# Down phases of four passes by a 26-product algorithm, with its w_down operands made beside earlier passes

## Chip, cores, metric

One core of a Trainium2 chip. The metric is the device time of one execution in microseconds (us).

## Reference

x is 8 x 1024 x 1024, w_gate and w_up 1024 x 4096, w_down 4096 x 1024, all fp32:

```python
gate = x @ w_gate
up = x @ w_up
gate = 0.5 * gate * (1 + np.tanh(np.sqrt(2 / np.pi) * (gate + 0.044715 * gate ** 3)))
h = gate * up
return (h @ w_down).astype(np.float32)
```

## The kernel before

Eight passes of 1024 tokens, counted from 0. Each pass has a gate/up phase and a down phase. Operands are fp16. The down phase multiplies h (1024 x 4096) by w_down with seven products of a Strassen scheme: 7 x 2 x 4 x 8 = 448 matmuls of 512 columns. I call 8 of them, one group below, a slot (1.73 us). Parts, with cuts marked "...":

```python
def cast_x(p):                      # fp32 -> fp16 through the DMA, on GpSimd's queue
    r = slice(p * TOK, (p + 1) * TOK)
    nc.gpsimd.dma_start(out=xh[r, :], in_=x2[r, :])

def transpose_x(p):                 # four DMA transposes, on SyncE's queue
    for n, kh, mh in (("b11", 0, 0), ("b21", 1, 0), ("b12", 0, 1), ("b22", 1, 1)):
        r0 = p * TOK + mh * MH
        nc.sync.dma_start_transpose(
            out=xq[n], in_=xh[r0 : r0 + MH, kh * MH : (kh + 1) * MH]
        )
...
def gate_up_fast(p):                # passes 3 to 7: 8 quads of 26 products of 8 matmuls
    owed = {}
    for q in range(NQ):
        extra = {}
        if q == 2 and p + 1 < NPASS:
            extra[3] = [lambda: cast_x(p + 1)]
        ...
DSEQ = ["P1", "P2", "P6", "P5", "P7", "P3", "P4"]
def down(p):
    ...
    for v, name in enumerate(DSEQ):
        ...
        for nb in range(2):
            kc = 2 * v + nb
            dc = d_chunk(p, kc)                     # w_down operand, in a ring of six chunks
            for g in range(G):
                for n in range(8):
                    nc.tensor.matmul(ps_all[:, bank[b, g]], lhs[...], dc[:, n, :], ...)
                ...
                if nb == 1:
                    if name == "P1":                # ScalarE copies bank a to bank c;
                        bank["c", g] = ps_free.popleft()   # P2 goes on in bank c
                        nc.scalar.copy(ps_all[:, bank["c", g]], ps_all[:, bank["a", g]])
                    ...
                for s in sums.get((name, nb, g), ()):
                    hsum(*s)                        # VectorE: sums of h
                if nb == 0 and g == 0 and p + 1 < NPASS:
                    ...
                    if v == (2 if p < FAST - 1 else 0):     # FAST = 3
                        transpose_x(p + 1)
                if v >= (5 if p < FAST - 1 else 3) and work:
                    work.popleft()()                # VectorE: scaling and sums of next x
            ...
                if kc == 0 and p < FAST:
                    for k in range(3, 6):
                        load_d(p, k)                # ring loads, SyncE's queue
                load_d(p, kc + 6)
```

All loads, stores and transposes but the casting ones are issued by SyncE, in program order. And ScalarE's copy from bank a to bank c stands between product P1 and product P2: TensorE needs it at slot 8, 13.8 us into the phase.

## Time and profile before

| | before |
|---|---|
| median of 3 runs | 2290.01 us (2289.75 to 2291.56) |
| TensorE in a down phase | 96.69 us, no wait |
| TensorE in a fast gate/up phase | 181.65 us, no wait |

The chain of the kernel before and its stages are in the prediction. One more view of it is needed: SyncE's timeline where down phase 2 begins (it begins at 795.30). Columns: start and duration in us, engine, line, operation, what is moved, how many.

```profile
795.37 8.98 SPq L178 DMA_TRANSPOSE x_b<-x_half  x4
804.45 11.92 SPq L396 DMA_DIRECT2D ring<-wd_ops  x6
```

The four transposes of the next x hold SyncE's queue for 9.0 us; the ring loads of the phase come behind them, and in time.

### The profile page before, as it was taken

Reading aid. Unit: us, or ns where it says so; the run is one execution under the profiler, and the core shown is the slowest. Engines: PE = TensorE matmul, PEld = TensorE weight load, DVE = VectorE, ACT = ScalarE, POOL = GpSimd, SP = SyncE. Lnnn points to the kernel's source line nnn. Section 1 sums busy time; section 2 is a strip of 40 time slices with the busy share of each in tenths; the row PEclk is TensorE's granted clock in tenths of the full one; section 3 lists DMA queues with packets and bytes.
Section 4 is the critical chain, followed back from the end, with each engine's and each line's share of the span. In section 5 each row is a group of like instructions: output and inputs, shape, how many; then the busy total and the mean of one; then the engine's idle time right before and its main releaser. Section 6 shows DMA issues by size and latency. Waiting matters only on the chain.

```text
span 2287.4 us, 38185 instructions
## 1 busy us (share of the span) xinstructions
PE 2276.5 (100%) x14719; PEld 1437.7 (63%) x14719; DVE 1342.2 (59%) x1946; ACT 958.6 (42%) x1860; POOL 676.4 (30%) x818
## 2 busy tenths in 40 slices
PE   9999999999999999999999999999999999999999
PEld 4444444444444446887468874788648886488854
DVE  5576367772587744677346673466735677256650
ACT  4443135551355513555135641455404553055620
POOL 1342013230133301454024540254303452044520
PEclk9999999999999999999999999999999999999999
DMA  9998959888899977988579885798858987588752
GB/s 239 175 207 211 254 144 225 215 255 250 182 220 225 266 245 258 308 287 263 203 263 317 275 275 193 265 319 277 268 194 273 311 284 253 198 279 281 268 210 108
DMA packets 258054, 557.20 MB, mean 244 GB/s; under 512 B 74768, under 2 KB 134160, under 8 KB 243728
## 3 DMA queue, kind: packets, MB, share of 16 engines
q1 hardware_dynamic: 204992, 483.46, 62.1%
q0 software_dynamic: 52880, 71.31, 18.8%
q8 instruction: 115, 1.88, 0.4%
q14 instruction: 67, 0.55, 0.1%
HBM read 512.75 MB, written 113.25 MB: 274 GB/s over the span
## 4 chain that ended last, share of the span: by engine, by line
PE 97%; DVE 2%; issue 0%; DMA 0%; ACT 0%; SPq 0%; DVEq 0%; ACTq 0%
PE ps L681 40%; PE ps L793 34%; PE ps L474 23%; PE ps L877 1%; DVE ring L273 1%; DVE tmp L493 0%; DMA h_a<-in_x_dram 0%; DVE h_a L511 0%; DVE x_sums L201 0%; DVE h_s L334 0%; DVE h_s L336 0%; DVE h_s L338 0%; ACT x_b L229 0%; DVE x_b L228 0%; SPq L217 0%
## 5 line engine op out<-in xcount | busy, mean ns | idle before, releaser
L681 PEld LDWEIGHTS <-ring 128*128 128x128 f16 x8320 | 814.1, 98 | 95.2
L658 POOL TENSOR_TENSOR h_a<-tmp 128x256 f16<-128x256 f32 x640 | 465.5, 747 | 927.4 <-ACT tmp L646 893.5
L681 PE MATMUL ps<-x_sums,ring 128*128 128x256 f16 x5760 | 655.8, 273 | 0.0
L793 PE MATMUL ps<-ring,h_a 128*128 128x512 f16 x2944 | 638.4, 379 | 0.0
L643 DVE TENSOR_TENSOR tmp<-tmp,ps 128x512 f32<-128x512 f32 x640 | 413.8, 683 | 220.4 <-PE ps L681 168.3
L793 PEld LDWEIGHTS <-h_a 128*128 128x128 f16 x3072 | 300.6, 98 | 361.4
L474 PEld LDWEIGHTS <-ring 128*128 128x128 f16 x2632 | 257.5, 98 | 314.5 <-issue 4.7
L628 ACT COPY tmp<-ps 128x512 f32<-128x512 f32 x520 | 304.4, 585 | 203.9 <-PE ps L681 128.9
L474 PE MATMUL ps<-x_sums,ring 128*128 128x512 f16 x1504 | 341.0, 379 | 3.0 <-DVE ring L273 2.0
L646 ACT ACTIVATE tmp<-tmp 128x256 f32<-128x256 f32 x640 | 263.8, 418 | 172.7 <-DVE tmp L641 80.0
L732 ACT ACTIVATE tmp<-ps 128x512 f32<-128x512 f32 x128 | 76.4, 597 | 587.2 <-PE ps L793 587.2
L681 PE MATMUL ps<-x_b,ring 128*128 128x256 f16 x2560 | 305.6, 273 | 0.0
L500 POOL TENSOR_TENSOR h_a<-tmp 128x512 f16<-128x512 f32 x94 | 150.4, 1600 | 375.1 <-ACT tmp L498 286.1
L474 PE MATMUL ps<-x_b,ring 128*128 128x512 f16 x1128 | 259.1, 379 | 0.0
L641 DVE TENSOR_TENSOR tmp<-ps,tmp 128x512 f32<-128x512 f32 x240 | 165.4, 689 | 151.4 <-ACT tmp L628 104.2
L736 DVE SCALAR_TENSOR_TENSOR tmp<-ps,tmp 128x512 f32<-128x512 f32 x64 | 44.2, 690 | 303.4 <-ACT tmp L732 260.3
L493 DVE TENSOR_TENSOR tmp<-ps,tmp 128x512 f32<-128x512 f32 x188 | 127.0, 683 | 137.5 <-ACT tmp L485 134.6
L485 ACT COPY tmp<-ps 128x512 f32<-128x512 f32 x188 | 110.1, 586 | 92.2 <-PE ps L474 89.7
L740 DVE TENSOR_TENSOR h_a<-h_a,h_a 128x2048 f16<-128x2048 f16 x96 | 111.2, 1215 | 58.1 <-PE ps L793 58.1
L273 DVE TENSOR_TENSOR ring<-ring 128x1024 f16<-128x1024 f16 x188 | 132.7, 721 | 6.9 <-PE ps L793 3.8
L498 ACT ACTIVATE tmp<-tmp 128x512 f32<-128x512 f32 x94 | 58.8, 626 | 146.6 <-DVE tmp L493 146.6
L793 PE MATMUL ps<-ring,h_s 128*128 128x512 f16 x480 | 104.9, 379 | 0.0
(68 smaller groups left out, 798.6 us busy)
## 6 DMA issues: line engine op xcount, KB each, us to landing
ring<-w_ops SPq DMA_DIRECT2D x480, 512.0 KB, 4.5
ring<-wd_ops SPq DMA_DIRECT2D x105, 1024.0 KB, 5.4
out_dram<-tmp SPq DMA_DIRECT2D x128, 256.0 KB, 2.5
w_ops<-x_sums SPq DMA_DIRECT2D x110, 256.0 KB, 6.3
ring<-in_w_gate_dram POOLq DMA_DIRECT2D x23, 1024.0 KB, 9.9
ring<-in_w_up_dram POOLq DMA_DIRECT2D x23, 1024.0 KB, 18.0
w_ops<-h_s SPq DMA_DIRECT2D x82, 256.0 KB, 5.5
x_half<-in_x_dram POOLq DMA_DIRECT2D x7, 2048.0 KB, 15.7
```

The lines of the kernel that those rows point to most:

```text
L273: nc.vector.tensor_tensor(o, a, b, op)
L474: nc.tensor.matmul(ps(b, w), lhs[:, k], rhs[:, k, :], start=(first and k == 0), stop=(k == KH - 1), skip_group_check=True,)
L493: nc.vector.tensor_tensor(o, ps("b", w), o, ADD)
L500: nc.gpsimd.tensor_tensor(hq[TO[n]][:, i, :], tmp[:, t[n, 1]], tmp[:, t[n, 0]], MUL)
L628: nc.scalar.copy(tmp[:, t[o[1]]], ps_all[:, bank[o[2]]])
L641: nc.vector.tensor_tensor(d, b, a, SUB)
L643: nc.vector.tensor_tensor(d, a, b, ADD if o[4] == "add" else SUB)
L646: nc.scalar.activation(d, d, GELU, scale=GSC)
L658: nc.gpsimd.tensor_tensor(h, tmp[:, t[o[1]], MQ : 2 * MQ], g, MUL)
L681: nc.tensor.matmul(ps_all[:, bank[c], w * MQ : (w + 1) * MQ], lhs[:, w, k], rhs[:, k], start=(first and w == 0 and k == 0), stop=(k == KH ...
L740: nc.vector.tensor_tensor(hq[o][:, s, :], hq[a][:, s, :], hq[b][:, s, :], op)
L793: nc.tensor.matmul(ps_all[:, bank[b, g]], lhs[:, j, g * P : (g + 1) * P], dc[:, n, :], start=(first and j == 0), stop=(j == NP - 1), skip_ ...
```

## The change

Intent: in passes 4 to 7 the down phase becomes `down_fast`, an algorithm with 26 products of 32 matmuls of 256 columns (832 matmuls) where the plain product of these blocks has 32. It needs 24 operands of 1 MB that are sums of blocks of w_down. They are made once, in eight units, beside passes 2 to 4: two units each in down phases 2 and 3 and in gate/up phases 3 and 4. The core of the diff, cut (the lists of sums and products and most of `down_fast` are left out):

```diff
+    def wd_unit(u, raw, free):
+        ...
+        def load():
+            for k, c, v in ((0, 0, 0), (1, 0, 1), (1, 1, 5)):
+                nc.sync.dma_start(out=blk[:, k, c], in_=wdop[2 * v + nb][:, j : j + 2, :])
+            nc.gpsimd.dma_start(out=blk[:, 0, 1], in_=wd_eo[0][:, 2 * u : 2 * u + 2, HH:])
+        ...
+        def step(i):                      # 19 of them
+            stores()                      # to DRAM, SyncE's queue
+            n, op, a, b = WD_SUMS[i]
+            v = at[n] = free.popleft()
+            combine(node(n), op, node(a), node(b))       # VectorE
+            ...
+            if i % 3 == 0 and i // 3 < len(plain):
+                m, sign = plain[i // 3]
+                v = free.popleft()
+                nc.scalar.activation(..., node(m), COPY, scale=float(sign))   # ScalarE
 ...
     def gate_up_fast(p):
+        if p in UNITS_UP:
+            free = deque(hf["s3"][:, 4096 + j * 512 : 4608 + j * 512] for j in range(8))
+            for i, u in enumerate(UNITS_UP[p]):
+                load, fs = wd_unit(u, hf["s3"][:, 0:4096], free)
+                steps[i * 78] = load
+                for k, f in enumerate(fs):
+                    steps[i * 78 + 14 + 3 * k] = f
 ...
+    UNITS_DOWN = {2: (0, 1), 3: (4, 5)}
+    UNITS_UP = {3: (2, 3), 4: (6, 7)}
 ...
     def down(p):
+        if p in UNITS_DOWN:
+            free = deque(xc[:, j * 512 : (j + 1) * 512] for j in range(24, 38))
+            for i, u in enumerate(UNITS_DOWN[p]):
+                load, fs = wd_unit(u, xc[:, i * 8192 : i * 8192 + 4096], free)
+                steps[i] = [load]
+                for k, f in enumerate(fs):
+                    steps.setdefault(3 + 19 * i + k, []).append(f)
 ...
                         if v == (2 if p < FAST - 1 else 0):
                             transpose_x(p + 1)
-                    if v >= (5 if p < FAST - 1 else 3) and work:
+                    for f in steps.get((2 * v + nb) * G + g, ()):
+                        f()
+                    if v >= x_from and work:
                         work.popleft()()
 ...
-        down(p)
+        if p < DFAST:                     # DFAST = 4
+            down(p)
+        else:
+            down_fast(p)
```

In a gate/up phase a slot is 8 matmuls of 256 columns, 0.873 us, and a phase has 208 of them.

## The prediction

> **What bounds the kernel now.** I read the list of the critical chain in order of time first, then the busy times of each engine by stage, then timelines of the moments where a down phase begins. The kernel has eight passes of 1024 tokens; each is a gate/up phase and a down phase. From pass 2 on (passes are counted from 0) the chain is nothing but TensorE:
>
> ```profile
> 795.30 96.69 PE ps L793 x448
> 891.99 181.65 PE ps L681 x1664
> 1073.65 96.69 PE ps L793 x448
> 1170.34 181.65 PE ps L681 x1664
> ...
> 2005.38 181.65 PE ps L681 x1664
> 2187.03 96.71 PE ps L793 x448
> ```
>
> Columns: start, duration, engine and line, instructions. L793 is a down phase (7 products, 448 matmuls of 512 columns), L681 a fast gate/up phase (1664 matmuls of 256 columns). Each piece starts where the last ended: no wait anywhere. So time saved in TensorE's instruction stream counts in full, and each new wait counts in full. From these rows, a 512-column matmul takes 96.69/448 = 0.2158 us, a 256-column one 181.65/1664 = 0.10917 us.
>
> The stages (passes 3, 5 and 7):
>
> ```profile
> core 0: us, PE busy (x) PEld busy (x) DVE busy (x) ACT busy (x) POOL busy (x), PEclk, DMA share, GB/s
> 891.99:1073.65 181.66, 181.66 (x1666) 162.77 (x1664) 120.37 (x190) 106.99 (x230) 88.28 (x125) 1.00 0.86 292
> 1351.99:1448.69 96.70, 96.70 (x451) 43.92 (x449) 41.74 (x50) 12.63 (x23) 5.31 (x5) 1.00 0.66 215
> 2187.03:2283.70 96.67, 96.67 (x449) 43.63 (x446) 26.87 (x27) 12.64 (x23) 5.32 (x5) 1.00 0.39 140
> ```
>
> VectorE (DVE) and the DMA are far from full in a down phase; in the gate/up phase the DMA share is 0.86. That is where the change has to find room.
>
> [...]halving the columns costs about 2.5 ns per extra matmul. [...]the trace's h sums of that size take 1215. [...]four such sums beside GpSimd take 5.87 us, eight without it 9.16 (1.47 against 1.15 each). [...]the busiest fortieth of this trace moves 319[...].
>
> **The change, part by part.**
>
> *TensorE.* A down phase of passes 4 to 7 becomes 26 products of 16 x 2 matmuls of 256 columns: 832 x 0.10917 = 90.83 us for 96.69. Saved 5.86 us a pass, 23.4 us in four. Weight loads (98 ns each) must hide under 109 ns, as they already do in L681. 2290.0 - 23.4 = 2266.6 is the floor.
>
> *VectorE in the new phase.* 18 sums of 128x4096 f16; none exists yet. Rows of 1024 and 2048 elements take 683 and 1215 ns, so an estimate by that slope is 2.28 us: 41.0 us. 24 reads of PSUM at 0.69: 16.6. 23 operations for the next pass's x (21 near 0.69, 2 of 1.22): 16.8. Together 74.4 of 90.8 us. A product lasts 32 x 0.109 = 3.49 us; by the program's list no slot holds more than about 3.0 us of VectorE work except two with 4.6, each with light neighbours, and each sum stands about one slot ahead of its use.
>
> *Start of that phase.* In pass 5 GpSimd is still multiplying h when the phase starts at 1351.99:
>
> ```profile
> 1350.49 6.81 POOL L658 TENSOR_TENSOR h_a<-tmp 128x256 f16<-128x256 f32 x7 [1.20 <-ACT tmp L646]
> ```
>
> It ends 5.3 us in. The first two products leave their last two rows for later: 56 matmuls, 6.1 us. That holds. The first sum waits for the fourth from last multiplication (some 2.5 us in) and the second for the last; they end near 5.5 and 8, and are needed at 10.5 and 14.0.
>
> *Making the operands.* Eight units, each 19 sums of 128x512 f16 (0.42 us, estimated from 683 - 266), six ScalarE copies (0.6), four loads and 24 stores of 128 KB. Two units go into the down phases of passes 2 and 3 and into the gate/up phases of passes 3 and 4. On average it fits: 16 us of VectorE on 120.4 of 181.7, or on 41 of 96.7. The order in the queues is what costs. In a down phase the first step stands at the end of slot 3 (a slot is 8 matmuls, 1.73 us), but its loads stand behind the x transposes in the sync engine's queue. The built program's waits say: ScalarE's copy of step 0 waits for the third of these loads; ScalarE runs in order; behind it is the PSUM copy that TensorE needs for the first matmul of P2 at slot 8, 13.8 us in. Pass 3, before:
>
> ```profile
> 1074.05 12.60 SPq L178 DMA_TRANSPOSE x_b<-x_half  x4
> 1086.75 7.97 SPq L396 DMA_DIRECT2D ring<-wd_ops  x3
> ...
> 1082.32 0.57 ACT L809 COPY ps<-ps 128x512 f32<-128x512 f32 x1 [6.54 <-PE ps L793]
> ```
>
> The transposes hold the queue until 13.0 us after the phase starts (1073.65). Three loads at 0.35 us of issue each, 2.5 to 3.5 us to land (loads of 512 KB land in 3.1 at best), 0.6 for the operand copy and 0.57 for the PSUM copy end near 18.3: a wait of about 4.5 us at 13.8. In pass 2 the transposes end 9.2 us in, so the same sum gives 14.5 to 15.5: about 1 us.
>
> In the gate/up phases the loads are early enough. But there a step meets GpSimd, busy half of the time[...]. Laid against the build's waits, the tightest release in a group of 26 products is the bank of the 18th, free 0.86 us before its matmul.[...] I allow 2 us for the two phases. For small waits at the starts of the four new phases I allow 1 us, and nothing for the tail (the last operation is one VectorE read for one ScalarE copy, then a store of the same size).
>
> Sum: 2266.6 + 4.5 + 1.0 + 2.0 + 1.0 = 2275.1; I say **2274.5**.
>
> **Rivals.**
> 1. *The DMA becomes the bound.* Loads go from 14 to 24 MiB a down phase: one of 1.05 MB per 3.49 us, 300 GB/s. With 4.2 MB of output (now rows of 1 KB) and 2.1 MB of transposes: 31.5 MB in 90.8 us, 347 GB/s. The rows above put the most at an estimated 280 to 360 (140 at a share of 0.39; 292 at 0.86). For it: no room inside the phase. Against it: over a whole pass it is (292 x 181.7 + 347 x 90.8)/272.5 = 310, and every load is issued five slots, 17.5 us, before its use while it lands in 5.4. The lag can grow to 12 us before TensorE sees it, and the gate/up phase pays it back. If the DMA gave only 300 GB/s: 105 us per phase, and the time near 2300 with nothing gained.
> 2. *VectorE becomes the bound.* If the sums took 3 us, its work would be 87 of 90.8 us and the chains of dependent sums would show: 3 to 8 us a pass, 2285 to 2300. Against it: GpSimd is idle there, so sums should run at the rate of the lone ones.
> 3. *No new wait.* ScalarE's wait in passes 2 and 3 is hidden because the loads land sooner: 2267 to 2269.
>
> **Range and chances.** The floor is safe to 1 us. The waits add 2 to 17 us: 2268 to 2284. A gain over 2% would need 2244, beyond what TensorE's stream can give: 0.01. A loss over 2% (2336) needs rival 1 at its worst: 0.02. Within 2%: 0.97.
>
> **What would show it.** Right: the chain has four pieces of 832 matmuls near 90.8 us, VectorE near 74 us busy in passes 4 to 6 and 58 in pass 7; pass 3's down phase has one wait of 3 to 6 us of TensorE for ScalarE at the first matmul of P2, pass 2's a smaller one; gate/up phases 5 to 7 stay at 181.65. Wrong: new phases over 93 us (releaser a load: rival 1; a VectorE sum: rival 2), down phases 2 and 3 at 96.7, or gate/up phases 3 and 4 longer by over 3 us each.

The 2.0 us for the gate/up phases rested on a cost per step whose source was not given; the 2.0 stands as an allowance. (Measured afterwards: a unit's sums in these phases took 0.42 us each at the median, 0.68 and 0.75 at the longest.) Measured in the kernel before: h sums of 128x2048 fp16 took 1215 ns each; at the start of pass 3's down phase four of them took 5.87 us, most of it beside GpSimd (the same four took 4.63 us without it in pass 2), and the eight behind them 9.16 us without it; and the busiest of the page's 40 slices moved 319 GB/s.

## The result, and the profile after

The changed kernel takes 2292.7 us (median of 4 runs, 2291.3 to 2298.8), the one before 2289.9 beside it. The ratio is 1.0017, 95% interval 0.9997 to 1.0036. A ratio here is the mean time of one kernel's fast runs over that of the other's of the same rounds, so not quite the ratio of the medians quoted. The time lies 18 us above what was predicted and outside the range.

The chain of the changed kernel in order of time (start, duration, engine and line, instructions). In it L965 is the old down phase, L1079 the new one, L827 a fast gate/up phase, L254 the transposes, L470 a unit's loads, L500 ScalarE's operand copy, L981 ScalarE's copy of bank a to bank c:

```profile
796.00 13.83 PE ps L965 x64
809.83 2.03 SPq L254
811.92 0.57 SPq L470
...
813.01 5.53 DMA x_sums<-wd_ops
...
819.10 0.59 ACT ps L981
819.73 84.60 PE ps L965 x384
...
1103.88 4.90 DMA x_sums<-wd_ops
1108.81 0.63 ACT x_sums L500
1109.44 0.49 ACT ps L981
1109.98 84.54 PE ps L965 x384
...
1377.41 90.83 PE ps L1079 x832
1468.23 181.65 PE ps L827 x1664
```

Read it backwards from 819.73: TensorE waited there for ScalarE's bank copy, that for a load of a unit, that for SyncE, and SyncE was still in the transposes. The same at 1109.98. The new phase has no wait: 90.83 us for 832 matmuls.

The stages of the changed kernel (columns as in the prediction's table of stages):

```profile
796.00:904.32 108.32, 98.41 (x451) 44.20 (x449) 53.57 (x87) 18.38 (x32) 3.41 (x4) 0.95 0.98 292
904.32:1087.90 183.58, 181.99 (x1666) 162.74 (x1664) 133.81 (x228) 110.83 (x242) 92.70 (x126) 1.00 0.95 332
1087.90:1194.52 106.62, 98.35 (x450) 44.23 (x449) 55.40 (x88) 18.80 (x35) 7.38 (x8) 0.97 0.93 277
1194.52:1377.41 182.89, 181.81 (x1666) 162.81 (x1665) 134.63 (x228) 110.81 (x242) 92.20 (x126) 1.00 0.97 344
1377.41:1468.23 90.82, 90.82 (x834) 81.39 (x833) 72.35 (x67) 8.45 (x16) 5.39 (x5) 1.00 0.98 312
```

Against 96.69 and 181.65 before: down phase 2 is 11.6 us longer, down phase 3 9.9, gate/up phase 3 1.9, gate/up phase 4 1.2. The four new phases are 5.86 us shorter each, 23.4 together. Passes 0 and 1 and the start of 2 took 0.7 us more, the tail 0.2 (passes 0 to 2 vary: over all the profiles, down phase 2 begins between 795.2 and 796.8). The sum is 11.6 + 9.9 + 1.9 + 1.2 + 0.7 + 0.2 - 23.4 = +2.1 us, and the spans differ by 2.1 (2289.5 and 2287.4). **So nothing of the gain was lost in the new phases; all of it was spent where the operands are made**, and 21.5 us of it in two down phases.

In those two phases TensorE waited 9.91 and 8.27 us. The rest, 1.7 us in each, is a lower clock. Two stretches just after the first wait, where the last three columns are the clock, the DMA share and GB/s:

```profile
819.73:823.20 3.47, 3.47 (x9) 1.23 (x9) 3.47 (x6) 2.51 (x5) 0.00 (x0) 0.54 1.00 414
823.20:826.70 3.50, 3.50 (x18) 1.59 (x17) 3.50 (x6) 0.00 (x0) 0.00 (x0) 1.00 1.02 424
```

In the first 3.47 us the granted clock is 0.54: 9 matmuls in the time of 16. In the next 3.50 us it is 1.00 again. The whole piece shows the same loss: the 384 matmuls behind the wait took 84.60 us where 384 x 0.2158 = 82.87.

Why was the queue held so long? SyncE's timeline of the changed kernel at the start of down phase 2 (796.00), to be laid beside the one of before:

```profile
796.08 15.79 SPq L254 DMA_TRANSPOSE x_b<-x_half  x4
811.92 3.33 SPq L470 DMA_DIRECT2D x_sums<-wd_ops  x6
815.36 2.51 SPq L529 DMA_DIRECT2D ring<-wd_ops  x4
```

The same four transposes take 15.8 us in place of 9.0. What differs is a second queue. This is the DMA traffic by queue in the stretch from 801 to 806 us (packets, MB, time that the packets took as a share of 16 engines); first before, then after:

```profile
q1 hardware_dynamic: 4702, 1.19, 117.9%
```

```profile
q1 hardware_dynamic: 817, 0.21, 76.2%
q0 software_dynamic: 264, 0.26, 52.8%
```

q0 is GpSimd's queue: the fourth load of each unit, which casts fp32 to fp16 on the way. Both units' casting loads are issued at once. While they move, the queue of the transposes gets through a sixth of the packets. A packet of it takes on average 0.762 x 16 x 5 us / 817 = 75 ns instead of 1.179 x 16 x 5 us / 4702 = 20 ns. At this point it is only a coincidence in time, so it is tested below.

### The profile page after: what moved, and what is told of

Its sections match the earlier page's. It is cut to its first block, busy times and chain, and to the rows that moved or that the text cites. A ratio compares the mean times of both kernels' runs of the same rounds, so it can differ in the third digit from the quotient of the medians.

```text
span 2289.5 us, 42138 instructions
## 1 busy us (share of the span) xinstructions
PE 2257.8 (99%) x16255; PEld 1589.1 (69%) x16255; DVE 1524.7 (67%) x2170; ACT 959.3 (42%) x1876; POOL 687.8 (30%) x826
## 4 chain that ended last, share of the span: by engine, by line
PE 93%; DMA 3%; DVE 2%; SPq 1%; issue 1%; ACT 0%; DVEq 0%; ACTq 0%
PE ps L827 38%; PE ps L620 22%; PE ps L965 16%; PE ps L1079 16%; DMA ring<-w_ops 1%; DVE ring L349 1%; SPq L254 1%; DMA h_s<-wd_ops 1%; PE ps L1178 1%; DVE x_sums L277 0%; DMA x_sums<-wd_ops 0%; DVE tmp L639 0%; DMA h_a<-in_x_dram 0%; DVE h_a L657 0%; DVE h_s L410 0%
## 5 line engine op out<-in xcount | busy, mean ns | idle before, releaser
L827 PEld LDWEIGHTS <-ring 128*128 128x128 f16 x8320 | 814.1, 98 | 97.8 <-issue 3.2
L804 POOL TENSOR_TENSOR h_a<-tmp 128x256 f16<-128x256 f32 x640 | 472.5, 758 | 787.3 <-ACT tmp L792 774.6
L827 PE MATMUL ps<-x_sums,ring 128*128 128x256 f16 x5760 | 655.9, 273 | 0.2 <-DVE tmp L789 0.2
L965 PE MATMUL ps<-ring,h_a 128*128 128x512 f16 x1408 | 308.9, 382 | 18.2 <-ACT ps L981 18.2
L827 PE MATMUL ps<-x_b,ring 128*128 128x256 f16 x2560 | 305.9, 273 | 2.5 <-DVE tmp L789 2.5
L965 PEld LDWEIGHTS <-h_a 128*128 128x128 f16 x1536 | 150.9, 98 | 202.0 <-issue 22.8
L1079 PEld LDWEIGHTS <-h_a 128*128 128x128 f16 x1792 | 175.4, 98 | 20.3
L1079 PE MATMUL ps<-ring,h_a 128*128 128x256 f16 x1536 | 172.9, 273 | 0.0
L1136 ACT ACTIVATE tmp<-ps 128x512 f32<-128x512 f32 x48 | 28.2, 597 | 290.1 <-PE ps L1079 219.7
L893 ACT ACTIVATE tmp<-ps 128x512 f32<-128x512 f32 x64 | 38.2, 597 | 265.9 <-PE ps L965 265.9
```

What stands on the lines that cost most here:

```text
L804: nc.gpsimd.tensor_tensor(h, tmp[:, t[o[1]], MQ : 2 * MQ], g, MUL)
L827: nc.tensor.matmul(ps_all[:, bank[c], w * MQ : (w + 1) * MQ], lhs[:, w, k], rhs[:, k], start=(first and w == 0 and k == 0), stop=(k == KH ...
L965: nc.tensor.matmul(ps_all[:, bank[b, g]], lhs[:, j, g * P : (g + 1) * P], dc[:, n, :], start=(first and j == 0), stop=(j == NP - 1), skip_ ...
L1079: nc.tensor.matmul(ps_all[:, bank[c], m * MQ : (m + 1) * MQ], lhs[:, j, m * P : (m + 1) * P], rhs[:, j, :], start=(first and j == 0 and m ...
```

## The experiments

Eleven kernels ran. The first table has their times (before beside them: 2288.7 in the first group of four, 2289.0 in the others), the second their stages, read off each chain. A wait in a stage is counted with what follows from it. Every ratio is within 2%; the intervals tell them apart. The stages come from one profiled execution of each kernel. The runs of e1 and e3 are up to 11 us apart, so their stages are those of one execution only.

| kernel | median us | lowest to highest | ratio to before, 95% interval |
|---|---|---|---|
| after | 2292.7 | 2291.3 to 2298.8 | 1.0017 [0.9997, 1.0036] |
| e1 unit loads first | 2286.2 | 2279.2 to 2289.9 | 0.9983 [0.9964, 1.0002] |
| e2 transposes late | 2272.7 | 2270.4 to 2274.2 | 0.9927 [0.9912, 0.9941] |
| e3 copies late | 2285.3 | 2278.1 to 2287.6 | 0.9977 [0.996, 0.9995] |
| e4 no casting loads (wrong result) | 2290.5 | 2287.2 to 2291.4 | 1.0003 [0.9986, 1.002] |
| e5 unit and ring loads first | 2274.1 | 2271.3 to 2274.7 | 0.9932 [0.9919, 0.9946] |
| e6 operands made, old down phases | 2314.4 | 2313.3 to 2314.9 | 1.011 [1.0096, 1.0124] |
| e7 transposes late, both units later | 2277.4 | 2275.3 to 2278.4 | 0.995 [0.9936, 0.9963] |
| e8 e1 without casting loads (wrong result) | 2286.8 | one run | state unknown |
| e9 loads behind two transposes | 2283.7 | one run | state unknown |
| e10 transposes late, second unit later | 2266.5 | 2265.6 to 2268.5 | 0.9903 [0.9889, 0.9916] |
| e11 transposes late, cast of x late | 2266.9 | 2265.6 to 2270.7 | 0.9905 [0.989, 0.992] |

| stage, us | before | after | e1 | e2 | e3 | e4 | e5 | e7 | e8 | e9 | e10 | e11 |
|---|---|---|---|---|---|---|---|---|---|---|---|---|
| down 2 | 96.7 | 108.3 | 111.8 | 96.7 | 104.4 | 103.2 | 98.4 | 96.7 | 103.6 | 103.4 | 96.7 | 96.7 |
| gate/up 3 | 181.7 | 183.6 | 183.3 | 185.0 | 191.6 | 186.4 | 183.0 | 184.9 | 187.2 | 184.9 | 181.7 | 181.7 |
| down 3 | 96.7 | 106.6 | 96.7 | 96.7 | 97.0 | 104.4 | 96.7 | 96.7 | 96.7 | 102.0 | 96.7 | 98.0 |
| gate/up 4 | 181.7 | 182.9 | 183.5 | 184.3 | 183.9 | 186.4 | 184.2 | 186.6 | 188.9 | 183.7 | 181.7 | 181.7 |

### e1: the unit loads ahead of the transposes

```diff
+                    for f in steps.get((2 * v + nb) * G + g, ()):
+                        f()
                     if nb == 0 and g == 0 and p + 1 < NPASS:
                         ...
                             transpose_x(p + 1)
-                    for f in steps.get((2 * v + nb) * G + g, ()):
-                        f()
```

> The three sync-queue loads of a unit are issued ahead of the four x transposes instead of behind them, nothing else moves. Theory (the queue order is the cause: loads stuck behind transposes that hold the queue 15 us, ScalarE in order behind its operand copy): the waits of TensorE in down phases 2 and 3 (9.9 and 8.3 us) go, both phases take 96.7 to 97.5 us instead of 108.3 and 106.6, and the whole takes 2270 to 2273 us, ratio to before about 0.992. Rival A (the loads are slow because the DMA engines are full there, whatever their place): the loads land 5 to 8 us late anyway and at least 5 us of each wait stay, total 2283 or more. Rival B (VectorE has too much work in these phases): phases stay above 105 us.

Half a hit, half a miss. Down phase 3 is back at 96.7, as the queue theory says. Down phase 2 is longer than ever, 111.8, so the total is 2286, not 2270 to 2273. The wait on ScalarE is gone there, and another has come. SyncE's timeline of e1 (the phase begins at 795.93), and TensorE's waits of that phase (us in all, times, longest):

```profile
795.99 1.34 SPq L470 DMA_DIRECT2D x_sums<-wd_ops  x3
797.76 21.46 SPq L254 DMA_TRANSPOSE x_b<-x_half  x4
...
820.90 3.30 SPq L529 DMA_DIRECT2D ring<-wd_ops  x4
```

```profile
PE ps L965 <- DMA ring<-wd_ops: 12.7, 1, 12.7
```

The transposes now hold the queue 21.5 us, and behind them stand the ring loads of chunks 3 to 5, needed from slot 12 on (96 matmuls in). In the changed kernel they were late too, but hidden: TensorE was waiting already. Two questions follow: are the ring loads the only thing left (e5), and what makes four transposes take 21.5 us (e4, e8)?

### e5: the ring loads ahead of the transposes too

```diff
 (e1, and behind its loop over steps:)
+                    if p in UNITS_DOWN and p < FAST and kc == 0 and g == 0:
+                        for k in range(3, 6):
+                            load_d(p, k)
 ...
-                    if kc == 0 and p < FAST:
+                    if kc == 0 and p < FAST and p not in UNITS_DOWN:
```

> The run with the unit loads first, and in down phase 2 also the three ring loads of w_down chunks 3 to 5 ahead of the transposes. In the run with the unit loads first, down phase 3 went back to 96.69 us but down phase 2 still took 111.8, with one wait of 12.7 us on a ring load that stood behind the transposes, which held the queue 21.5 us. Theory (in down phase 2 two kinds of loads stood behind the transposes, and taking one ahead only showed the other): the ring wait goes, down phase 2 takes 96.7 to 98.5 us, the whole 2270 to 2274 us, ratio about 0.992. Rival (the DMA engines cannot carry transposes, casting loads and ring loads in that time in any order): a wait of 4 us or more stays in down phase 2, total 2277 or more.

As expected: 2274.1, down phase 2 about 98.4 us, with 1.4 us of waits left on VectorE, and down phase 3 at 96.7. The transposes still held the queue for 21.7 us; nothing that TensorE needs soon stood behind them any more.

### e2: the transposes at slot 16

```diff
-                        if v == (2 if p < FAST - 1 else 0):
+                        if v == (2 if p < FAST - 1 or p in UNITS_DOWN else 0):
                             transpose_x(p + 1)
```

> The same cause from the other side: in passes 2 and 3 the x transposes are issued at slot 16 of the down phase instead of slot 0, so that the loads find the sync queue free. Theory: the first waits go as in the run with the loads first, but now the unit's stores and the ring loads stand behind the transposes for 9 to 15 us, so some wait may come back elsewhere: phases of 96.7 to 100 us, total 2270 to 2277. Rival A: phases above 103 us, total 2283 or more.

The same cause from the other side, and a one-line mend: 2272.7. Both down phases are without a wait. The chain of e2 there:

```profile
796.17 96.69 PE ps L965 x448
892.86 68.72 PE ps L827 x630
...
1077.91 96.69 PE ps L965 x448
```

The fear that stores and ring loads behind the later transposes would bring a new wait was not borne out. With e1 and e5 this settles that the order in SyncE's queue made both waits. Rival A (slow loads wherever they stand) and rival B (too much work for VectorE) are wrong for these phases: e2 has the same VectorE work (53.1 and 55.2 us) in 96.69 us.

### e3: ScalarE's operand copies later

```diff
-            if i % 3 == 0 and i // 3 < len(plain):
-                m, sign = plain[i // 3]
+            if i >= 6 and i % 2 == 0 and i // 2 - 3 < len(plain):
+                m, sign = plain[i // 2 - 3]
```

> The queue stays as it is and the loads land as late as before; only the six ScalarE operand copies of a unit move from steps 0, 3, 6, .. to steps 6, 8, .. 16, that is behind ScalarE's four PSUM copies. Theory (ScalarE in order is what carries the late load to TensorE): the waits on the PSUM copy go in both phases though the load still lands at 18 to 23 us into the phase. VectorE still stands at step 0 till then, so the sum that the third product needs at 27.7 us may be a little late in down phase 2: a wait of 0 to 3 us on VectorE there. Down phases 97 to 101 us, total 2270 to 2277. Rival (the late load itself, through VectorE's sums, holds TensorE): waits of 8 us stay, now on VectorE.

The loads stay as late as before. In down phase 3 the wait is gone (97.0 us): so it is ScalarE's place in order, not the late load as such, that carried it to TensorE. In down phase 2 the wait on ScalarE is gone as well, but TensorE then met the late ring load, 5.9 us, where I had expected up to 3 us on VectorE. The total missed the expected 2270 to 2277 for this reason and because `wd_unit` is shared with the gate/up phases: in gate/up phase 3, where only eight buffers are free, bunched copies met a store of the unit that took 14.9 us to land, and the phase took 191.6.

### e4 and e8: no casting loads (wrong result)

```diff
-            nc.gpsimd.dma_start(out=blk[:, 0, 1], in_=wd_eo[0][:, 2 * u : 2 * u + 2, HH:])
+            nc.sync.dma_start(out=blk[:, 0, 1], in_=wdop[8 + nb][:, j : j + 2, :])
```

e4 is the changed kernel with this edit, e8 is e1 with it.

> Wrong result on purpose: the fourth load of each unit, a casting load of 512 KB of w_down from fp32 by GpSimd's queue, is replaced by a sync-queue load of 256 KB of another fp16 operand, issued last of the four. It tests what held the transposes in down phase 2 for 15.8 us instead of the 9.0 us of the kernel before. Theory[...]: the four transposes of pass 3's x in down phase 2 hold the queue 9 to 10 us again, TensorE's wait there falls from 9.9 to 2 to 4.5 us; in down phase 3, where one cannot tell how much of the 14.5 us it is, the hold falls by 1 to 3 us and the wait from 8.3 to 5 to 7. Total 2279 to 2287. Rival (the hold is longer for another reason, for example the loads still in flight from the phase before): the hold stays at 15 us and the waits at 8 to 10 us.

> Wrong result on purpose: unit loads ahead of the transposes, and the casting load by GpSimd's queue replaced by a sync-queue load of half the bytes. Tests whether the casting loads are what made the transposes hold the queue 21.5 us in the run with the loads first. Theory: the transposes in down phase 2 hold it 10 to 13 us, the ring loads behind them come in time or 1 to 3 us late, and down phase 2 takes 96.7 to 101 us in place of 111.8. Rival: the hold stays above 18 us and the wait above 9 us.

How long the four transposes held the queue in down phase 2, from SyncE's timelines:

| ahead of the transposes | with casting loads | without |
|---|---|---|
| nothing | 15.8 (after) | 10.6 (e4), 9.0 (before) |
| the first unit's loads | 21.5 (e1) | 12.3 (e8) |

The lines of e4 and of e8:

```profile
795.33 10.60 SPq L254 DMA_TRANSPOSE x_b<-x_half  x4
798.73 12.29 SPq L254 DMA_TRANSPOSE x_b<-x_half  x4
```

So it is no coincidence: **without the units' casting loads beside them, the transposes of down phase 2 hold the queue 5 to 9 us less**. Two other kernels show how firm the sizes are. e3 and e6 leave this queue as the changed kernel has it, and the hold was 14.5 and 14.0 us, so against e4 the difference is 3 to 5 us. e5 has the order of e1, and its hold was 21.7. In down phase 3, where the changed kernel issued the casting loads 4.8 us behind the first transpose instead of 2.1, the effect is smaller: 14.5 (after) against 12.0 (e4), and 16.9 (e1) against 12.6 (e8).

What these two runs do not separate: the edit takes away the cast, GpSimd's queue and half of the bytes read, all at once, and puts the new loads behind the transposes (in e8 only that of the second unit), where the casting loads did not stand. Which of these held the transposes stays open.

In e4 the hold of 10.6 us is a little over the 9 to 10 that I had said; TensorE's wait in down phase 2 fell from 9.9 to 4.6 (I had said 2 to 4.5), in down phase 3 from 8.3 to 6.3, the hold there from 14.5 to 12.0 us. In e8 the ring wait fell from 12.7 to 4.3, where I had said at most 3, and down phase 2 took 103.6 where I had said at most 101; the direction is right, the sizes a little off. The total of e4, 2290.5, missed the expected 2279 to 2287. The totals are not better because these two kernels lost 3 to 6 us more than the changed kernel did in gate/up phases 3 and 4 each, where the replaced load stands in SyncE's queue as a fourth one. I did not follow that up.

### e9: a dose

```diff
+                            if p in UNITS_DOWN:
+                                transpose_x(p + 1, slice(0, 2))     # two, then the unit's loads,
+                            else:
+                                transpose_x(p + 1)                  # then the other two
                     for f in steps.get((2 * v + nb) * G + g, ()):
                         f()
+                    if p in UNITS_DOWN and (v, nb, g) == (0, 0, 0):
+                        transpose_x(p + 1, slice(2, 4))
```

> A dose: the loads of a unit stand behind two of the four transposes instead of all four. Theory (the wait is as long as the time the transposes ahead of the loads hold the queue, plus the landing of the load): in down phase 2 the first two transposes held it about 11 us, in down phase 3 about 9 us, so the waits on the PSUM copy fall from 9.9 and 8.3 us to 4 to 6.5 and 1.5 to 5 us; the loads in flight may lengthen the last two transposes, and the ring loads behind those may be late in down phase 2 as in the run with the loads first. Rival: waits unchanged. The clock after such shorter waits is open: if it falls only after a long idle time, TensorE's 384 matmuls take 82.9 us again, else 84.5.

In down phase 3 the wait fell from 8.3 to 3.5, within the expected. In down phase 2 it fell to 1.3, less than expected, as the first two transposes held the queue only 7.1 us; the late ring load came in its place (3.4). The clock fell after both waits of 3.4 to 3.5 us: it was 0.52 in the 3.5 us behind each, and 1.00 in the 4 us after that.

### e6: the operands made, the old down phases kept

```diff
-    DFAST = 4
+    DFAST = 8
```

> The operands are made as in the change, but no pass uses the new down phase (one constant): all eight have 448 matmuls of 512 columns. Theory (the saving is 5.86 us a phase, taken out of the chain whole, and the making costs what the stages 2 to 4 show, 25 us): 23.4 us more than the changed kernel, 2314 to 2318 us, ratio to before 1.011. Rival (the new phases cost something that the chain does not show, or the making costs less where its operands are not read): under 2311.

2314.4, as expected at its lower end, 21.8 us above the changed kernel's median; the four down phases took 96.69 to 96.71 again. The exchange is additive within 2 us: the new phases gave their 23.4 us, the making costs about 25 (here 24.2 by the stages: 9.6 and 10.4 in the down phases, 1.4 and 2.6 in the gate/up phases, 0.3 ahead of down phase 2; in the changed kernel 25.5).

### e7, e10, e11: what stays in the gate/up phases

e2's gate/up phases 3 and 4 are still 3.4 and 2.6 us too long. There ScalarE and VectorE stood at the second unit's first step: its loads, due at slot 78, landed 16 to 18 us later, and the step stood 12.2 us behind. e7 has e2's edit and moves both units:

```diff
-                steps[i * 78] = load
+                steps[i * 88] = load
-                    steps[i * 78 + 14 + 3 * k] = f
+                    steps[i * 88 + 26 + 3 * k] = f
```

> Two mends: transposes of passes 2 and 3 at slot 16 (as in the run that has it alone, which took 2272.7), and in gate/up phases 3 and 4 the first step of a unit 26 slots (22.7 us) behind its loads instead of 14 (12.2 us), the second unit's loads at slot 88 instead of 78. In the run with the transposes late the two gate/up phases took 185.0 and 184.3 us, with waits of TensorE on VectorE's accumulation where VectorE and ScalarE stood at a unit's step for a load that landed 16 to 18 us behind its slot. Theory: these waits go, both phases take 181.7 to 182.3 us, the whole 2266.5 to 2269 us, ratio about 0.990. Rival (the extra work of VectorE and ScalarE in these phases costs it whatever the place): 2271 or more.

A miss: 2277.4, slower than e2. The chain of e7 in gate/up phase 3, and the landing times of what was issued from 941 to 960 us (the last column, us):

```profile
945.50 0.52 DVE h_s L277
946.02 13.68 DMA wd_quads<-h_s
...
960.89 117.22 PE ps L827 x1072
```

```profile
x_half<-in_x_dram POOLq DMA_DIRECT2D x1, 2048.0 KB, 15.2
wd_quads<-h_s SPq DMA_DIRECT2D x6, 128.0 KB, 13.6
```

The first unit, 12 slots later, was in the middle of its work when the cast of the next x began (slot 55, GpSimd's queue again, 2 MB): a store took 13.7 us to land, and VectorE waited for its buffer. So the place matters, and a casting load moved beside it again. Two ways out of that, each on top of e2. e10 leaves the first unit and delays only the second unit's steps by 8 slots; e11 leaves both and moves the cast behind them:

```diff
 e10
-                    steps[i * 78 + 14 + 3 * k] = f
+                    steps[i * 86 + 14 + 3 * k] = f
 e11
-            if q == 2 and p + 1 < NPASS:
+            if q == (6 if p in UNITS_UP else 2) and p + 1 < NPASS:
```

> Transposes of passes 2 and 3 at slot 16, and only the second unit's first step in gate/up phases 3 and 4 eight slots (7 us) later, behind loads that landed 17.8 us after their slot. With both units later the waits moved to a store of the first unit that took 13.7 us to land while the cast of the next x moved; the first unit stays in place here. Theory (the gate/up waits are those of a step for a load not landed): both gate/up phases take 181.7 to 182.6 us instead of 185.0 and 184.3, the whole 2266.5 to 2270 us. Rival (any place for the steps meets a store or a load that is late, as the DMA engines are busy 96 to 98% of these phases): 2271 us or more.

> Transposes of passes 2 and 3 at slot 16, units at their places, but in gate/up phases 3 and 4 GpSimd's casting load of the next x (2 MB) is issued in the seventh quad, behind all unit work, instead of the third. Theory (it is this cast, 15 us long, that made the second unit's loads and the first unit's stores late): the landing of those loads falls below 12 us, the waits go, both gate/up phases take 181.7 to 182.6 us, the whole 2266.5 to 2270 us. Rival (the ring loads ahead of the unit's loads in the sync queue make them late, cast or not): 184 us stay, the whole 2271 or more.

Both come to the floor: 2266.5 and 2266.9, gate/up phases of 181.65 to 181.68. The chain of e10:

```profile
795.79 96.69 PE ps L965 x448
892.49 181.68 PE ps L827 x1664
1074.17 96.69 PE ps L965 x448
...
1352.54 90.83 PE ps L1079 x832
```

Nothing but TensorE from down phase 2 to the end. In e11 SyncE issued the second unit's loads of gate/up phase 3 at 961.35, at their slot, within 1.4 us; in e2, where the cast moved at that time, it came to them 5.1 us later (966.45) and needed 4.5 us. With the cast elsewhere the steps stay where the change put them and no wait is left. (e11 has 1.3 us in down phase 3, 1.0 of it waits on VectorE; I do not know whether that recurs.) e10 is faster than both kernels, by 1.0% against before (0.9889 to 0.9916); the diff of this version is the change plus two lines.

## Why the prediction was wrong, point by point

**The floor and the new phases: right.** 832 x 0.10917 = 90.83 was said, 90.82 to 90.84 measured; 23.4 us saved, and e10 at 2266.5 stands near the floor of 2266.6 (22.5 us under the 2289.0 measured beside it). VectorE was said to be busy 74 us in passes 4 to 6 and 58 in pass 7; it was 72.4 in pass 4's down phase and 57.4 in the last. Rival 1 (the DMA the bound) did not come true: the share was 0.98 at 312 GB/s, but TensorE never waited; the loads were early enough. Nor was 0.98 the end of what the DMA can do: a stretch shown above moved 424 GB/s at a share of 1.02, and the kernel before moved 426 GB/s from 815 to 819 us. The 319 GB/s that the prediction took from the page were an average over a fortieth of the span, 57 us. Rival 2 (VectorE the bound) did not come true either: TensorE never waited for it there. The 1.0 us for the starts of the new phases was not needed.

**The mechanism in down phases 2 and 3: right.** ScalarE's operand copy waited for a load that stood behind the transposes, and the bank copy behind it held the first matmul of P2. e1, e2, e5 and e9 break that chain in SyncE's queue, e3 on ScalarE.

**Its sizes: wrong, and this is the step that failed.** "A wait of about 4.5 us" in down phase 3 was 8.27 us, and "about 1 us" in down phase 2 was 9.91, so the phase that was said to wait less waited more. Each term of the sum, with what it measured:

| term | said, phase 3 | measured | said, phase 2 | measured |
|---|---|---|---|---|
| transposes hold the queue until | 13.0 us | 14.8 | 9.2 us | 15.9 |
| the third load lands after | 2.5 to 3.5 us | 4.9 | 2.5 to 3.5 us | 5.5 |
| first matmul of P2 | near 18.3 us | 22.1 | 14.5 to 15.5 us | 23.7 |
| clock after the wait | none | 1.7 us | none | 1.7 us |

The first term was read from the kernel before and carried over, though the change puts casting loads beside those same transposes, and though phase 2 of that kernel was the shortest hold of its seven. That was most of the error in phase 2, and e4 and e8 show what it came from: 10.6 and 12.3 us without these loads, 15.8 and 21.5 with them. The second term was near the best case of a load; the DMA share in these phases was 0.98 and 0.93. The clock was not thought of: each of the two waits was followed by 1.7 us more. Together 11.6 + 9.9 where 1.0 + 4.5 were set down: 16.0 us, nearly the whole of the error of 18.2 (2292.7 - 2274.5).

**The gate/up phases: near in size, wrong in cause.** 2 us were allowed, for steps that meet GpSimd; 3.2 came. The prediction held that "the loads are early enough" there. They were not: e2's second unit had its loads 16 to 18 us behind their slot, and moving either the step (e10) or the cast of x (e11) took the waits away. No run speaks for GpSimd as the cause.

**Rival 3 (no new wait)** is what e10 is, two edits later.

**Slips in the working.** The stage at 1351.99 is pass 4's down phase, not pass 5's; its numbers are read rightly. With 9.2 us for the transposes the prediction's own terms give 13.9 to 14.9 us for phase 2, not 14.5 to 15.5. Its 105 us a phase at 300 GB/s would be 57 us more in four phases, so a time near 2330 and not 2300, unless the gate/up phases paid it back. The 280 at the lower end of "280 to 360" GB/s comes from neither row that it names; they give 340 and 360.

## What to carry to other kernels

A load added to an in-order queue must be costed with what stands ahead of it and with the transfers that the same change puts beside that, not with the old kernel's timeline. A mend can show a wait that the first one hid (e1), so look for every transfer that stands behind the same holder. A wait of TensorE can cost clock as well: behind 16 of 17 waits of 3.0 to 12.7 us in these runs the matmuls took 1.5 to 3.0 us more than their usual time (an estimate from the pieces of their chains, last section); and where a phase has little slack, an instruction on an in-order engine should stand behind the latest landing of its load, or the traffic that makes the load late should move.

## What else the runs measured

- Two casting loads of GpSimd's queue (each reads 512 KB of fp32) beside four DMA transposes: the transposes held SyncE's queue for 14.0 to 15.8 us instead of 10.6, and 21.5 instead of 12.3. While a casting load of a whole x moved (2 MB written), stores of 128 KB took 13.6 us to land (e7, 941 to 960 us); with that load elsewhere they took 5.1 (e11, 940 to 992 us).
- Four transposes of 512 x 512 fp16 held their queue 9.0 us at the best (down phase 2 of the kernel before), from 795.37 to 804.35; the first ring load behind them stands at 804.45.
- A stream of 448 matmuls of 512 columns ran at 215.8 ns each, streams of 1664 and 832 of 256 columns at 109.2 ns.
- The clock behind waits of TensorE. The third column is the granted clock in the 6.0 us behind the wait, where that was asked. The last is an estimate: the piece of the chain behind the wait, less its number of matmuls times 0.2158 or 0.10917 us. (e3's wait of 5.7 us in gate/up phase 3 is left out, as its piece could not be told apart.)

| kernel, phase | wait, us | clock behind it | lost, us |
|---|---|---|---|
| after, down 2 and 3 | 9.9, 8.3 | 0.73, 0.74 | 1.7, 1.7 |
| e1, down 2 | 12.7 | 0.62 | 2.4 |
| e3, down 2 | 5.9 | not asked | 1.9 |
| e4, down 2 and 3 | 4.6, 6.3 | 0.72, 0.78 | 1.9, 1.5 |
| e4, gate/up 3 and 4 | 3.0, 3.2 | not asked | 1.9, 1.5 |
| e6, down 2 and 3 | 7.7, 8.5 | not asked | 1.9, 1.9 |
| e7, gate/up 3 and 4 | 3.1, 3.3 | 1.00, 0.75 | 0.2, 1.7 |
| e8, down 2, gate/up 3 and 4 | 4.3, 3.7, 4.3 | not asked | 2.6, 1.8, 3.0 |
| e9, down 2 and 3 | 3.4, 3.5 | 0.52 in 3.5 us; in 6.0 us 0.72, 0.72 | 1.9, 1.8 |

One wait of 3.1 us (e7) left the clock at 1.00, and one of about 3.0 (e4) was followed by a loss of 1.9; what decides that was not shown. Behind two shorter waits, 1.3 us in e9 and 2.6 in e2, the clock was 1.00 in the next 4.0 and 3.5 us. This was worked out from the traces afterwards; no run was made for it.
